# A hybrid transformer block: the second norm beside the attention, with its squares in two halves on ScalarE, its scaling on GpSimd and its transposes in groups of four

## The chip, the cores and the metric

The kernel runs on one core of one Trainium2 chip. The metric is the device time of one launch in microseconds (us). Every time below comes from the runs of the kernel before or from one profiled execution of it.

## The reference

One encoder block over 2048 tokens of width 1024, all in float32. What the change touches is the second norm, `h2`, and the attention that runs at the same time:

```python
h = rmsnorm(x, norm1_g) * (1.0 + sc1) + sh1
proj = h @ w_in                                  # 8 query heads, 2 key/value heads of 64, 512 pool channels
att = blocked_gqa(q, k, v)                       # softmax over all 2048 keys
pool = pool_mixer(u_pool, w_pool, pool_scale)
x = x + g1 * (jnp.concatenate([att, pool], -1) @ w_out)
h2 = rmsnorm(x, norm2_g) * (1.0 + sc2) + sh2     # y = x * rsqrt(mean(x*x) + 1e-6), per token
x = x + g2 * conv_gated_ffn(h2, w_up, conv_w, conv_b, w_down)
```

## The kernel before

The kernel has three stages: the first norm and the input projections (to about 380 us), the attention (380 to 1240 us), and the gated MLP (to the end). Matrices are split into a high and a low float32r part, so that most products take two or three matmuls.

**The attention** works through 32 *units*, numbered 0 to 31: a unit is one head for one chunk of 512 queries, chunk by chunk, 8 heads each. `gen_unit` goes over 16 key tiles. For each, TensorE makes a 128x512 tile of scores in PSUM with two matmuls (L731, and L732 which adds the row of maxima through `qb`), ScalarE takes the exponential twice (L735 into `ph`, L736 in place in PSUM), VectorE subtracts the two (L737, `pl`), and two tiles later TensorE multiplies by the values (L723 into bank `A`, L724 into bank `B`). GpSimd adds the `ph` of the first 13 tiles into `acc` (L739, then L741 eleven times). At the end of the unit ScalarE copies `acc` to `ah` (L751), VectorE makes its low part `al` (L752), and TensorE adds both into `B` (L757, L758); ScalarE and VectorE empty `A` and `B` (L765 to L768). For the next unit `gen_max` runs alongside: 16 matmuls (L692), each reduced by VectorE (L694), then the maxima as a row (L701), which ScalarE copies into `qb` (L702). The first L732 of a unit cannot start before that copy.

**Fillers.** Beside each unit a generator of other work is stepped at a fixed rate, which `count` (L913) sets: in units 8 to 15 the output projection (`gen_out`: matmuls L824, additions L846, loads L843, stores L847), in units 16 to 31 the second norm of token tiles 0 to 11 between further output projections. A scheduler then orders each engine's instructions by readiness, so a filler's instructions can stand some units before the place where they were written; the norm of tiles 0 and 1 starts in units 13 and 14.

**The second norm of a tile** (`ln2_early`, then `gen_ln2`, with 128 tokens): a load of x1 from DRAM into the buffer `l` (L879); ScalarE squares all 1024 columns and sums them (L853, an ACTIVATE and a short read of the accumulator); GpSimd makes the reciprocal root (L120, L121); VectorE scales the row in place (L857); a DMA copies it into a second buffer (L859); 8 transposes on TensorE into one PSUM bank, four at a time (L867), each four emptied by a ScalarE copy (L870) and stored (L871). Each buffer exists once, so the load of tile t+1 waits for the copy L859 of tile t, and that copy waits for the transposes of tile t-1. After `gen_ln2`'s first and second step come 4 and 8 empty steps (`LW`). Tiles 12 to 15 take the same function with `xr` None, in the turn from attention to MLP.

Every engine takes its own instructions strictly in order, and SyncE's queue (SP) issues all DMAs named here in order.

Of the kernel before, what the change touches and what calls it, by code (L numbers as in the profile page):

```python
# [10 lines left out]
F32 = mybir.dt.float32  # L11
F32R = mybir.dt.float32r
BF16 = mybir.dt.bfloat16
AF = mybir.ActivationFunctionType
ALU = mybir.AluOpType
# [3 lines left out]
P = 128  # L19
# [45 lines left out]
def hybrid_block(ctx: ExitStack, tc: tile.TileContext, x, c, w_ada, b_ada, norm1_g, w_in,  # L65
# [3 lines left out]
    V, S, G, PE, SP = nc.vector, nc.scalar, nc.gpsimd, nc.tensor, nc.sync  # L69

    x = x.rearrange("b t d -> (b t) d")
    out = out.rearrange("b t d -> (b t) d")
# [45 lines left out]
    def rstd_of(pool, ss, n, inv):  # L118
        r = pool.tile([P, n], F32, tag=f"rstd{n}", name="rstd", bufs=2)
        G.tensor_scalar(out=r, in0=ss, scalar1=inv, scalar2=EPS, op0=ALU.mult, op1=ALU.add)  # L120
        G.tensor_tensor(out=r, in0=r, in1=mhalf[:, 0:n], op=ALU.pow)  # L121
        return r
# [508 lines left out]
    with tc.tile_pool(name="po", bufs=1, side="right", reuse_waits="tile") as po, \  # L631
# [217 lines left out]
        def gen_ln2(t, x1, junk, hts, bank, stat, wait, xr=None):  # L849

            tok = t * P
            ss = stat.tile([P, 1], F32, tag="ss2", name=f"ss2{tok}", bufs=2)
            S.activation(out=junk(), in_=x1, func=AF.Square, accum_out=ss)  # L853
            r = rstd_of(stat, ss, 1, 1.0 / D)
            for _ in range(wait[0]):
                yield
            V.tensor_scalar(out=x1, in0=x1, scalar1=r, scalar2=None, op0=ALU.mult)  # L857
            if xr is not None:
                SP.dma_start(out=xr.bitcast(F32), in_=x1)  # L859
            for _ in range(wait[1]):  # L860
                yield
            src, eye = (x1, ident) if xr is None else (xr, identr)
            for q in range(2):
                tp = bank(f"tp2{tok}_{q}")
                for i in range(4):
                    k = q * 4 + i
                    PE.transpose(out=tp[:, i * P:(i + 1) * P], in_=src[:, k * P:(k + 1) * P], identity=eye)  # L867
                    yield
                hv = hts(q)
                S.copy(out=hv, in_=tp if xr is None else tp.bitcast(F32))  # L870
                SP.dma_start(out=h2_scr[4 * q:4 * q + 4, :, tok:tok + P].rearrange("k p t -> p k t"),  # L871
                             in_=hv.rearrange("p (k t) -> p k t", t=P))
                yield

        def ln2_early(t):
            xt, junk, xr, ht = (pw.tile([P, 2, QC], F32R, tag=f"mix{i}", name=f"l{i}_{t}", bufs=1)
                                .rearrange("p g t -> p (g t)") for i in ("00", "01", "10", "11"))
            xt, junk, ht = xt.bitcast(F32), junk.bitcast(F32), ht.bitcast(F32)
            SP.dma_start(out=xt, in_=x1_scr[t * P:(t + 1) * P])  # L879
            yield from gen_ln2(t, xt, lambda: junk, lambda q: ht[:, q * 512:(q + 1) * 512],  # L880
                               lambda nm: ps2.tile([P, 512], F32R, tag="misc", name=nm, bufs=1), p2, LW, xr)

        LW = (4, 8)
# [12 lines left out]
        def gen_first():  # L896
            mix3.extend(load_mix(NC - 1))
            for _ in range(12):
                yield
            yield from gen_tail_pool((("misc", 1), ("mx", 2), ("mx", 2)), mix3)  # L900
# [9 lines left out]
                2: lambda: chain(*(ln2_early(t) for t in range(4)), gen_out(1, 0), ln2_early(4), ln2_early(5)),  # L910
                3: lambda: chain(ln2_early(6), ln2_early(7), gen_out(2, 0), *(ln2_early(t) for t in range(8, 12)),
                                 gen_first())}
        count = {0: 2 * 96 + 12, 1: 192, 2: 96 + 6 * (10 + sum(LW)), 3: 96 + 6 * (10 + sum(LW)) + 48}  # L913
        filler = iter(())
        frac = 0.0
        FU, PT = 1, 1
# [151 lines left out]
        def gen_tail_att():  # L1068
            src = by_k(att.pop(NC - 1))
            for t in range(4):  # L1070
                tok = (NC - 1) * QC + t * P
                x1 = pv.tile([P, D], F32, tag=f"y{t}", name=f"x1{tok}", bufs=1)
                SP.dma_start(out=x1, in_=x[tok:tok + P])
                for n in range(2):
                    ns = slice(n * 512, (n + 1) * 512)
                    ps = tails[2 * t + n]
                    yield from gen_half(ps, src, 0, t, n, False, True)
                    V.tensor_tensor(out=x1[:, ns], in0=ps, in1=x1[:, ns], op=ALU.add)
                SP.dma_start(out=x1_scr[tok:tok + P], in_=x1)
                aux.append(gen_ln2(tok // P, x1, lambda: raw2("junk").bitcast(BF16),  # L1080
                                   lambda q: raw2("ht"), lambda nm: bank(nm), pa, TW[t]))
                step(aux[-1])

        def bank(nm):
            if ps3:
                return ps3[0].tile([P, 512], F32, tag="py", name=nm, bufs=3)
            return ps2.tile([P, 512], F32, tag="S", name=nm, bufs=3)
# [353 lines left out]
```

## Time and profile before

| | |
|---|---|
| median of 3 runs | 2693.97 us (2693.17 to 2694.17) |
| the profiled execution's own time | 2694.36 us |
| its span, first to last instruction | 2692.6 us |
| TensorE matmul busy | 2582.2 us, 96% of the span |
| VectorE busy | 1924.9 us, 71% |
| ScalarE busy | 1545.3 us, 57% |
| GpSimd busy | 1619.3 us, 60% |

The profiled execution is 0.39 us above the median, and 1.76 us of it lie outside the span. Matmul records overlap in time (each is shown from its start to its modelled end), so a busy share of 99% means that matmuls follow each other without a pause. In the records PE is TensorE, PEld its weight loads, DVE is VectorE, ACT is ScalarE, POOL is GpSimd, SPq SyncE's queue.

### The profile page before, as it was taken

What the parts mean: (1) busy time and instruction counts of PE and PEld (TensorE: products, weight loads), DVE (VectorE), ACT (ScalarE), POOL (GpSimd) and SP (SyncE); (2) the same over time, 40 slices, a digit from 0 to 9 for tenths busy, and PEclk for the clock granted to TensorE, in tenths of its full rate; (3) what the DMA queues carried; (4) which work ended last, traced back from release to release, by engine and by line L of the source; (5) the groups of instructions that cost most, each with busy time, mean ns of one, the idle gap of its engine ahead of it and who ended that gap; (6) DMA issues with size and microseconds to landing.
All of it is one profiled execution on the core that took longest, in us unless ns stands there. A gap on an engine that the chain in (4) does not pass through costs nothing.

```text
span 2692.6 us, 39012 instructions
## 1 busy us (share of the span) xinstructions
PE 2582.2 (96%) x13439; PEld 2238.4 (83%) x13439; DVE 1924.9 (71%) x3014; ACT 1545.3 (57%) x2848; POOL 1619.3 (60%) x1397
## 2 busy tenths in 40 slices
PE   5899989999999999999899999899999999999999
PEld 5788877777776777767898999799999997999998
DVE  7877678889988999897577776745555556455554
ACT  5565447767777778786654555554343445544442
POOL 1222135656566657574887887586565676777773
PEclk9899989999999999999999999999999999999999
DMA  9785373431223232333544444633333325333332
GB/s 293 237 265 180 97 240 101 153 100 58 69 73 98 64 100 62 97 110 120 172 149 134 149 130 140 197 106 102 106 105 95 94 78 189 114 122 118 107 112 87
DMA packets 320016, 344.90 MB, mean 128 GB/s; under 512 B 24975, under 2 KB 226649, under 8 KB 319817
## 3 DMA queue, kind: packets, MB, share of 16 engines
q1 hardware_dynamic: 318809, 338.60, 39.7%
q0 software_dynamic: 1008, 3.81, 0.5%
q8 instruction: 105, 1.72, 0.3%
q14 instruction: 94, 0.77, 0.1%
HBM read 249.42 MB, written 86.63 MB: 125 GB/s over the span
## 4 chain that ended last, share of the span: by engine, by line
PE 47%; DVE 2%; POOL 1%; ACT 1%; issue 1%; DMA 0%; DVEq 0%; SPq 0%; POOLq 0%; ACTq 0%
PE py L1254 16%; PE px L1165 13%; PE pw L1165 9%; PE pz L1165 8%; PE pl L1383 1%; DVE b L999 0%; POOL wl_s L1041 0%; ACT hb L983 0%; DVE y L1259 0%; DMA h_scr<-ht 0%; POOL wl_a L1041 0%; POOL t L1006 0%; POOL t L1013 0%; DMA hb<-h_scr 0%; DVE ac L1227 0%
## 5 line engine op out<-in xcount | busy, mean ns | idle before, releaser
L741 POOL TENSOR_TENSOR acc<-acc,ph 128x512 f32<-128x512 f32 x352 | 463.3, 1316 | 44.5 <-ACT ph L735 20.1
L1041 POOL TENSOR_TENSOR wl_s<-s,wh_s 128x512 fp32r<-128x512 f32 x260 | 349.4, 1345 | 204.7 <-ACT wh_s L1039 202.1
L735 ACT ACTIVATE ph<-S 128x512 fp32r<-128x512 f32 x512 | 306.8, 599 | 135.3 <-PE S L732 123.5
L737 DVE TENSOR_TENSOR pl<-S,ph 128x512 fp32r<-128x512 f32 x512 | 348.5, 684 | 40.5 <-ACT S L736 34.7
L1259 DVE TENSOR_TENSOR y<-py,y 128x512 f32<-128x512 f32 x300 | 205.9, 688 | 222.2 <-PE py L1254 220.6
L694 DVE TENSOR_REDUCE mx<-pmx 128x1 f32<-128x512 f32 x500 | 338.4, 681 | 21.1 <-PE pmx L692 19.5
L1039 ACT CAST wh_s<-s 128x512 fp32r<-128x512 f32 x264 | 163.5, 621 | 312.5 <-PE pw L1165 147.8
L1041 POOL TENSOR_TENSOR wl_a<-wr,wh_a 128x512 fp32r<-128x512 f32 x195 | 266.9, 1375 | 104.4 <-ACT wh_a L1039 104.0
L736 ACT ACTIVATE S<-S 128x512 f32<-128x512 f32 x512 | 306.0, 598 | 0.0
L1254 PE MATMUL py<-wdh,gh 128*128 128x512 f32 x664 | 261.7, 395 | 1.9 <-DVE y L1259 1.7
L1254 PE MATMUL py<-wdh,gl 128*128 128x512 f32 x664 | 262.0, 395 | 0.0
L1254 PE MATMUL py<-wdl,gh 128*128 128x512 f32 x664 | 261.8, 394 | 0.0
L1039 ACT CAST wh_a<-wr 128x512 fp32r<-128x512 f32 x198 | 122.3, 618 | 240.9 <-PE pz L1165 196.8
L1165 PE MATMUL px<-t,wh_s 128*128 128x322 f32 (+1 forms) x1024 | 248.0, 322 | 5.4 <-ACT p1s L1198 3.7
L724 PE MATMUL B<-pl,vt 128*128 128x512 f32 x512 | 209.9, 410 | 5.3 <-DVE pl L737 5.1
L732 PE MATMUL S<-qb,kB 65*128 65x512 f32 x512 | 203.3, 404 | 7.9 <-ACT qb L702 7.7
L692 PE MATMUL pmx<-kA,qa 128*128 128x512 f32 x500 | 204.9, 411 | 5.5 <-DMA kA<-k_scr 2.7
L723 PE MATMUL A<-ph,vt 128*128 128x512 f32 x512 | 204.4, 408 | 2.4 <-ACT ph L735 2.2
L731 PE MATMUL S<-qa,kA 128*128 128x512 f32 x512 | 202.7, 398 | 0.0
L1165 PEld LDWEIGHTS px<-t,wh_s 128*128 128x128 f32 x1024 | 178.3, 189 | 12.4 <-ACT p1s L1198 4.5
L739 POOL TENSOR_TENSOR acc<-ph,ph 128x512 f32<-128x512 f32 x32 | 41.2, 1288 | 239.2 <-ACT ph L735 209.2
L120 POOL TENSOR_SCALAR rstd<-ss 128x1 f32<-128x1 f32 (+1 forms) x48 | 20.5, 427 | 240.8 <-ACT junk L276 99.0
(297 smaller groups left out, 7034.4 us busy)
## 6 DMA issues: line engine op xcount, KB each, us to landing
wr<-in_w_up_dram SPq DMA_DIRECT2D x132, 512.0 KB
wdh<-wd_scr SPq DMA_DIRECT2D x88, 256.0 KB
wdl<-wd_scr SPq DMA_DIRECT2D x88, 256.0 KB
stage<-in_w_ada_dram SPq DMA_DIRECT2D x36, 512.0 KB
x_scr<-x SPq DMA_DIRECT2D x48, 256.0 KB
wds<-in_w_down_dram SPq DMA_DIRECT2D x44, 256.0 KB
wd_scr<-wdh SPq DMA_DIRECT2D x44, 256.0 KB
wd_scr<-wdl SPq DMA_DIRECT2D x44, 256.0 KB
```

Source lines behind the costliest of these rows:

```text
L692: PE.matmul(ps, qa[:, qt * P:(qt + 1) * P], kA[:, a, j * 512:(j + 1) * 512], start=True, stop=True)
L694: V.tensor_reduce(out=mx[:, qt, j:j + 1], in_=ps, axis=AX.X, op=ALU.max)
L724: PE.matmul(B, vt[:, kt, 64 + 64 * a:192 + 64 * a], pl, start=kt == 0, stop=False)
L735: S.activation(out=ph, in_=s, func=AF.Exp, scale=0.125)
L736: S.activation(out=s, in_=s, func=AF.Exp, scale=0.125)
L737: V.tensor_tensor(out=pl, in0=s, in1=ph.bitcast(F32), op=ALU.subtract)
L741: G.tensor_tensor(out=acc, in0=acc, in1=ph.bitcast(F32), op=ALU.add)
L1039: S.copy(out=hf, in_=src)
L1041: eng.tensor_tensor(out=lf, in0=src, in1=hf.bitcast(F32), op=ALU.subtract)
L1165: mm = PE.matmul(ps, l_[:, k], r_[:, k, 0:N], start=first and k == 0 and m == 0, stop=k == 3 and m == 2, skip_group_check=not first)
L1254: PE.matmul(ps, l_[:, ts_], r_, start=i == 0, stop=i == 3 * len(js) - 1)
L1259: V.tensor_tensor(out=ys[t][:, ns], in0=ps, in1=ys[t][:, ns], op=ALU.add)
```

## The change

For the twelve tiles beside the attention (`xr` not None) the squares are taken in two halves of 512 columns with two steps behind the first and one behind the second, and a GpSimd addition joins the two sums; the scaling moves from VectorE to GpSimd. For all 16 tiles the four transposes of a bank are issued in one step where each had a step of its own. A tile so takes 19 steps where it took 22, and `count`, from which the rate of the steps comes, follows. Lines from here on move by 10 in the changed kernel (L857 becomes L867, L879 becomes L889).

```diff
         def gen_ln2(t, x1, junk, hts, bank, stat, wait, xr=None):
 
             tok = t * P
-            ss = stat.tile([P, 1], F32, tag="ss2", name=f"ss2{tok}", bufs=2)
-            S.activation(out=junk(), in_=x1, func=AF.Square, accum_out=ss)
+            if xr is None:
+                ss = stat.tile([P, 1], F32, tag="ss2", name=f"ss2{tok}", bufs=2)
+                S.activation(out=junk(), in_=x1, func=AF.Square, accum_out=ss)
+            else:
+                s2, j2 = stat.tile([P, 2], F32, tag="ss2h", name=f"ss2h{tok}", bufs=2), junk()
+                for i in range(2):
+                    hs = slice(512 * i, 512 * (i + 1))
+                    S.activation(out=j2[:, hs], in_=x1[:, hs], func=AF.Square, accum_out=s2[:, i:i + 1])
+                    for _ in range(2 - i):
+                        yield
+                ss = s2[:, 0:1]
+                G.tensor_tensor(out=ss, in0=ss, in1=s2[:, 1:2], op=ALU.add)
             r = rstd_of(stat, ss, 1, 1.0 / D)
             for _ in range(wait[0]):
                 yield
-            V.tensor_scalar(out=x1, in0=x1, scalar1=r, scalar2=None, op0=ALU.mult)
+            (V if xr is None else G).tensor_scalar(out=x1, in0=x1, scalar1=r, scalar2=None, op0=ALU.mult)
...
                 for i in range(4):
                     k = q * 4 + i
                     PE.transpose(out=tp[:, i * P:(i + 1) * P], in_=src[:, k * P:(k + 1) * P], identity=eye)
-                    yield
+                yield
...
-        count = {0: 2 * 96 + 12, 1: 192, 2: 96 + 6 * (10 + sum(LW)), 3: 96 + 6 * (10 + sum(LW)) + 48}
+        count = {0: 2 * 96 + 12, 1: 192, 2: 96 + 6 * (7 + sum(LW)), 3: 96 + 6 * (7 + sum(LW)) + 48}
```

The order of the instructions is the same up to unit 12 and differs in small ways to the end of the turn into the MLP. Three places matter to the prediction.

*The end of unit 13.* First SyncE's queue, before and now (`l_1` with four digits is the x1 buffer of tile 1, `qa` and `qb` are query loads of unit 16, `o` and `rc` the row sums of unit 13):

```order
L847 DMA x_scr<-x_1_0_8178 128x512
L843 DMA x_1_0_8444<-x_scr 128x512
L680 DMA qa_8183<-q_scr 128x512
L681 DMA qb_8184<-q_scr 64x512
L879 DMA l_1_9241<-x_scr 128x1024
L774 DMA r_scr<-o_8429 1x512
```

```order
L847 DMA x_scr<-x_1_0_8178 128x512
L843 DMA x_1_0_8444<-x_scr 128x512
L889 DMA l_1_9230<-x_scr 128x1024
L680 DMA qa_8183<-q_scr 128x512
L681 DMA qb_8184<-q_scr 64x512
L847 DMA x_scr<-x_0_0_8327 128x512
```

Then ScalarE at the same place, before and now:

```order
L751 CAST ah_8407<-acc_8148 128x512
L765 COPY o_8429<-A_8149 64x512
L766 COPY o_8429<-B_8150 1x512
L853 ACTIVATE l_1_9242,ss_9246<-l_1_9241 128x1024
L702 CAST qb_7587<-row_8414 1x512
L735 ACTIVATE ph_0_8454<-S_0_8451 128x512
```

```order
L751 CAST ah_8407<-acc_8148 128x512
L765 COPY o_8429<-A_8149 64x512
L859 ACTIVATE l_1_9231,ss2h_9235<-l_1_9230 128x512 x2
L702 CAST qb_7587<-row_8414 1x512
L766 COPY o_8429<-B_8150 1x512
L735 ACTIVATE ph_0_8454<-S_0_8451 128x512
```

The load of tile 1 stands two DMAs earlier. Both halves of its squares stand one behind the other; before and now they are ahead of the copy into `qb`, and now they are also ahead of the copy of bank `B`.

*The end of unit 15*, ScalarE, before and now (tile 2):

```order
L765 COPY o_9002<-A_8745 64x512
L870 COPY l_1_9244<-tp_0_9357 128x512
L870 COPY l_1_9244<-tp_1_9406 128x512
L766 COPY o_9002<-B_8746 1x512
L853 ACTIVATE l_2_9456,ss_9460<-l_2_9455 128x1024
L702 CAST qb_8184<-row_8989 1x512
L735 ACTIVATE ph_0_9020<-S_0_9017 128x512
```

```order
L765 COPY o_9002<-A_8745 64x512
L880 COPY l_1_9233<-tp_0_9375 128x512
L880 COPY l_1_9233<-tp_1_9410 128x512
L859 ACTIVATE l_2_9432,ss2h_9436<-l_2_9431 128x512
L766 COPY o_9002<-B_8746 1x512
L702 CAST qb_8184<-row_8989 1x512
L859 ACTIVATE l_2_9432,ss2h_9436<-l_2_9431 128x512
L735 ACTIVATE ph_0_9020<-S_0_9017 128x512
```

One half now stands ahead of the copy of bank `B`, the other behind the copy into `qb`.

*The end of unit 16*, GpSimd, before and now (`acc_9014` is unit 16's):

```order
L120 TENSOR_SCALAR rstd<-ss_9663 128x1
L121 TENSOR_TENSOR rstd<-rstd,mhalf 128x1
L741 TENSOR_TENSOR acc_9014<-acc_9014,ph_8_9146 128x512
L741 TENSOR_TENSOR acc_9014<-acc_9014,ph_9_9162 128x512
L741 TENSOR_TENSOR acc_9014<-acc_9014,ph_10_9180 128x512
L741 TENSOR_TENSOR acc_9014<-acc_9014,ph_11_9198 128x512
L802 TENSOR_TENSOR attl_7126<-att_8898,atth_7125 128x512
L741 TENSOR_TENSOR acc_9014<-acc_9014,ph_12_9214 128x512
```

```order
L741 TENSOR_TENSOR acc_9014<-acc_9014,ph_11_9198 128x512
L863 TENSOR_TENSOR ss2h_9639<-ss2h_9639 128x1
L120 TENSOR_SCALAR rstd<-ss2h_9639 128x1
L121 TENSOR_TENSOR rstd<-rstd,mhalf 128x1
L867 TENSOR_SCALAR l_3_9634<-l_3_9634,rstd 128x1024
L802 TENSOR_TENSOR attl_7126<-att_8898,atth_7125 128x512
L741 TENSOR_TENSOR acc_9014<-acc_9014,ph_12_9217 128x512
```

The scaling of tile 3 stands ahead of unit 16's last addition. Of the twelve scalings seven stand in the gap behind a unit's last addition and five within a unit's additions: in units 16 (tile 3, before the last one), 19 (tile 4, after the ninth), 23 (tile 7, after the tenth), 26 (tile 8, after the fifth) and 29 (tile 11, after the seventh).

## Rows read from the trace of the kernel before

**Rows 1.** Windows: busy us (instructions) of PE, PEld, DVE, ACT, POOL; clock; DMA share, GB/s

```profile
440.00:735.00 295.00, 291.90 (x1258) 228.52 (x1258) 267.04 (x438) 215.75 (x401) 179.89 (x138) 1.00 0.32 100
735.00:970.00 235.00, 226.29 (x957) 169.62 (x956) 212.06 (x349) 179.10 (x337) 147.13 (x121) 0.98 0.28 82
970.00:1200.00 230.00, 221.81 (x958) 164.12 (x956) 209.15 (x348) 182.80 (x348) 145.31 (x120) 1.00 0.32 97
```

**Rows 2.** Timeline, unit 13 into 14: start, us, engine, line, operation [idle before <-releaser]

```profile
759.80 0.32 SPq L843 DMA_DIRECT2D x<-x_scr  x1
...
762.29 1.69 SPq L879 DMA_DIRECT2D l<-x_scr  x1
...
765.34 0.39 PE L758 MATMUL B<-al,onesr 128*128 128x512 f32 x1
...
767.84 1.06 ACT L853 ACTIVATE l<-l 128x1024 f32<-128x1024 f32 x1 [1.50 <-DMA l<-x_scr]
...
769.01 0.57 ACT L702 CAST qb<-row 1x512 fp32r<-1x512 f32 x1
...
769.64 0.73 PE L732 MATMUL S<-qb,kB 65*128 65x512 f32 x2 [1.93 <-ACT qb L702]
```

**Rows 3.** Windows, the stretches behind the two long stalls

```profile
769.70:773.40 3.70, 3.70 (x11) 2.90 (x12) 3.42 (x7) 3.09 (x6) 1.69 (x3) 0.61 0.20 68
826.00:831.00 5.00, 5.00 (x12) 3.45 (x12) 4.52 (x8) 3.09 (x6) 2.55 (x2) 0.50 0.30 109
```

**Rows 4.** Timeline, unit 15 into unit 16

```profile
818.07 0.50 SPq L879 DMA_DIRECT2D l<-x_scr  x1
...
822.17 0.69 DVE L768 TENSOR_TENSOR o<-B,o 64x512 f32<-64x512 f32 x1 [1.04 <-ACT o L766]
...
823.64 0.50 PE L692 MATMUL pmx<-kA,qa 128*128 128x512 f32 x1 [1.77 <-DVE mx L694]
823.91 1.06 ACT L853 ACTIVATE l<-l 128x1024 f32<-128x1024 f32 x1 [1.77 <-DMA l<-x_scr]
...
825.09 0.57 ACT L702 CAST qb<-row 1x512 fp32r<-1x512 f32 x1
...
825.71 1.65 PE L732 MATMUL S<-qb,kB 65*128 65x512 f32 x3 [1.56 <-ACT qb L702]
...
828.22 1.27 POOL L739 TENSOR_TENSOR acc<-ph,ph 128x512 f32<-128x512 f32 x1 [2.25 <-ACT ph L735]
```

**Rows 5.** Waits, 735 to 1200 us: us in total, times, longest

```profile
PE S L732 <- ACT qb L702: 7.1, 7, 1.9
```

**Rows 6.** Groups by line: busy us, mean ns | idle before

```profile
L741 POOL TENSOR_TENSOR acc<-acc,ph 128x512 f32<-128x512 f32 x352 | 463.3, 1316 | 44.5 <-ACT ph L735 20.1
L857 DVE TENSOR_SCALAR l<-l,rstd 128x1024 f32<-128x1024 f32 x12 | 9.2, 767 | 6.7 <-POOL rstd L121 6.5
L736 ACT ACTIVATE S<-S 128x512 f32<-128x512 f32 x512 | 306.0, 598 | 0.0
L102 POOL MEMSET onesz<- 128x192 f32 x1 | 0.3, 253 | 0.0
```

**Rows 7.** Timeline, the last addition and the copy `ah`: units 16, 19 and 23

```profile
846.84 1.29 POOL L741 TENSOR_TENSOR acc<-acc,ph 128x512 f32<-128x512 f32 x1
848.46 0.64 ACT L751 CAST ah<-acc 128x512 fp32r<-128x512 f32 x1
...
921.99 1.29 POOL L741 TENSOR_TENSOR acc<-acc,ph 128x512 f32<-128x512 f32 x1
923.83 0.61 ACT L751 CAST ah<-acc 128x512 fp32r<-128x512 f32 x1
...
1025.28 2.66 POOL L741 TENSOR_TENSOR acc<-acc,ph 128x512 f32<-128x512 f32 x2
1028.23 0.60 ACT L751 CAST ah<-acc 128x512 fp32r<-128x512 f32 x1
```

**Rows 8.** Timeline, the turn into the MLP: the first transpose of tile 12

```profile
1282.67 0.47 PE L867 MATMUL tp<-ident,x 128*128 128x128 f32 x1 [5.27 <-DVE x L857]
```

## The prediction

> **What bounds the kernel now.** I read the windows first, because the change lives between 735 and 1200 us. In the attention before it TensorE is busy for 291.90 of 295 us, with 1258 matmuls in that time, 0.232 us each [rows 1]: there it is the bound. In the two stretches with the second norm it is busy for 226.29 of 235 and 221.81 of 230 us: 8.7 and 8.2 us without a matmul, where the first stretch's rate would leave 2.5 each. Some 12 us of pauses, and a clock of 0.98 in the first stretch, are all that this part has to give. VectorE stands at 90% to 91% in all three, so it is close behind TensorE, and ScalarE and GpSimd are below 80%: what delays TensorE there is order and latency more than any engine's sum.
>
> Then the timeline, for where the pauses are. Two are long. **Unit 13 into 14** [rows 2]: the load of tile 1 is issued at 762.29; ScalarE, with the squares next in its queue, waits 1.50 us for it, squares from 767.84, and only at 769.01 copies the row into `qb`; TensorE stands 1.93 us until the first L732. The granted clock is 0.61 in the next 3.7 us [rows 3], so 0.39 x 3.7 = 1.4 us of TensorE's time go as well. **Unit 15 into 16** [rows 4]: the same with tile 2, where ScalarE waits 1.77 us, TensorE 1.77 and then 1.56 us, and the clock is 0.50 for 5 us [rows 3], the lower of TensorE's two levels (1.2 GHz of 2.4): another 2.5 us. The waits by group show that L732 waited for `qb` seven times, 7.1 us in all [rows 5]; without the two long ones (1.93 and 1.56) five remain, with 3.6 us together.
>
> Last, who is late at a unit's end. In unit 16 GpSimd's last addition ends at 846.84 + 1.29 = 848.13 and the copy `ah` starts at 848.46; the gaps are 0.33 us there, 0.55 in unit 19 and 0.29 in unit 23 [rows 7]. In these units GpSimd's chain of 12 additions already sets the end.
>
> **The change, part by part.** Durations are from the profiled execution, and the sum is made against its 2694.36 us, which is 0.39 above the median.
>
> *Squares at unit 14.* The load now follows L843, issued at 759.80 + 0.32, so some 2.1 us earlier than 762.29; with the same 5.55 us to the squares (762.29 to 767.84) the data are there at about 765.7. A half is priced by the 128x512 exponential, 0.60 us [rows 6], and 0.1 for the read of the sum (767.84 to 769.01 is 1.17 for a square of 1.06): 0.70, two of them 1.4. `qb` then starts at 767.1 and L732 at 767.7, 1.9 us earlier. But TensorE has four matmuls fewer ahead of that L732 than before (three where seven stood), 0.93 us that it must do later: the pause shrinks by 1.0, to about 0.95. Does the clock still fall? The five short waits, 0.7 us each, did not lower it (four of them lie in the second stretch of [rows 1], at 1.00), 1.93 us did; 0.95 is nearer to the short ones, so I take three quarters of the 1.4. Term: **-2.1 us**; ends: 0 (the load is no earlier) and -3.4 (pause and clock loss gone).
>
> *Squares at unit 16.* The load of tile 2 waits for the copy of tile 1, and that for tile 0's transposes, which now end about one key tile sooner (three units from 848.46 to 923.83 [rows 7], 18 steps each: 1.4 us): the data at 822.5 instead of 823.91. Then the first half (0.70), the copy of `B` (0.57, as the copy into `qb`), VectorE's L768 (0.69) and the reduction behind it (as long) stand in line before the L692 that TensorE must do ahead of L732. That L692 comes at about 825.1, where it came at 823.64, and L732 at 825.4 instead of 825.71: one wait takes the place of another. At the unit's end the scaling of tile 3 stands ahead of GpSimd's last addition. Term: **0**; ends: -5.8 (the pauses of 3.3 and the clock's 2.5 vanish) and +1.4 (the scaling's upper price below).
>
> *Fillers at the other starts of units.* In the order of the changed kernel three of the five short waits have two or three projection matmuls or four transposes ahead of L732: 3 x 0.7 = 2.2 us; as these units are not bound by TensorE throughout, two thirds: **-1.4** (ends 0 and -2.2).
>
> *Scaling off VectorE.* 12 x 0.767 = 9.2 us of VectorE's time go [rows 6]. In units full of projection matmuls TensorE hides them. Six tiles (2, 3, 6, 7, 10, 11) lie in units with few of them, 4.6 us; since a unit waits by turns for VectorE, ScalarE and GpSimd there, a third: **-1.5** (ends 0 and -4.6).
>
> *Scaling on GpSimd.* No row shows a GpSimd operation with one input of 1024 columns. Above, two inputs at 1.316 us for 512 columns make 2.63 [rows 6]; below, VectorE's own 0.767; GpSimd's fill of 192 columns in 0.253, in proportion, makes 1.35. A scaling streams one tensor, as the fill does, so I take 1.3. Seven scalings stand in the gap behind a unit's last addition, where GpSimd waits for the next unit's exponentials in any case (2.25 us at 828.22 [rows 4]); they cost nothing while they fit. Of the five within a unit's additions two have slack to spare, unit 16 is counted above, and in units 19 and 23 the addition of sums (0.2) and the scaling exceed the gaps: 0.2 + 1.3 - 0.55 = 1.0 and 0.2 + 1.3 - 0.29 = 1.2. In unit 28 the root moves behind the last addition, about -0.6. Term: **+1.6**; at 2.63 it is 1.3 more in each of the two and 1.0 in unit 29, +5.2.
> The Trainium skill (GPSIMD Engine Reference, section 4.1, Engine selection) speaks against the move: elementwise work on a tile belongs on VectorE, GpSimd being about twice as slow with two inputs and roughly at line rate with one. Twice VectorE's duration, an estimate by that page, is 1.53 us and would add 0.5 us to the sum; line rate would take 1.1 us off. No run here shows which holds.
>
> *Squares in two pieces.* 12 x (1.4 - 1.17) = 2.8 us more for ScalarE; it is last in perhaps a third of these units: **+0.9** (ends 0 and 2.8).
>
> *Grouped transposes.* In the order before, most transposes of a bank already stood by threes and fours, so nothing is counted (ends 0 and -1). In the turn into the MLP the first transpose of tile 12 waits 5.27 us for VectorE's L857 [rows 8], which is not changed, and the groups only come nearer to it: 0 (ends -2 and +2). What must also stay hidden: the copy L869 now waits in SyncE's queue for GpSimd instead of VectorE, with the row sums' DMAs behind it; late row sums would stop VectorE at L798.
>
> Sum: -2.1 + 0 - 1.4 - 1.5 + 1.6 + 0.9 = -2.5. 2694.36 - 2.5 = 2691.9, as a median **2691.5 us**: no change that a measurement could tell, as that takes about 0.2%, 5.4 us.
>
> **The rivals.** *Both long pauses go.* If the loads land before ScalarE comes to the squares, unit 14 gives 3.4, the short waits 2.2, VectorE 2.5; unit 16 gives 3.5 of its 5.8 before GpSimd's chain holds it: -11.6 + 1.6 + 0.9 = -9.1, a median of 2684.9. For it: both pauses begin with a wait for a load, and the order moves one load up. Against: tile 2's load stands at the same place in its queue, and the first half now delays the copy of `B`. Chance 0.36.
>
> *GpSimd's chain becomes the end of the units.* With the scaling near 2.63 us the terms are +1.4 (unit 16), +5.2 and, as ScalarE's copy `ah` then waits with the halves ahead of it, the full +2.8; the gains shrink to 1.0, 1.0 and 0.5: +6.9, a median of 2700.9. Three units follow the scaling's price one for one, so the sum is zero from about 2.1 us on. For it: gaps of 0.3 us, and the price of all two-input rows. Against: one input. Chance 0.22.
>
> *The halves do not interleave.* For tiles 0, 1 and 9 the scheduler put both in one place, so that they stop ScalarE for 1.4 us where one square took 1.17. That lies in the forecast's terms; if it were so everywhere, the first term falls away: 2693.6, still no change.
>
> **How the numbers follow.** No change has 0.42 (the forecast with the last case), faster 0.36, slower 0.22. The range 2682 to 2700 takes in the first rival with some room for the unit-16 term, and stops just short of the second's middle; the forecast's own is 2688 to 2697.
>
> **What would show it.** In the changed profile: the wait of L732 at the start of unit 14 near 1 us and full clock behind it; at the start of unit 16 L692 waiting for a reduction until after the copy of `B`, and a low clock still; the GpSimd TENSOR_SCALAR at 1.0 to 1.6 us; `ah` close behind the last addition in units 16, 19 and 23; TensorE's busy share in 735 to 1200 us at 97%. A scaling over 2 us, or a unit 16 under 27 us, would make the forecast wrong, to either side.

## The result, and the profile after

The changed kernel takes 2718.68 us as the median of four runs (2717.22 to 2720.07), against 2693.57 us for the kernel before on the same chip: a ratio of 1.0096, 95% interval 1.0084 to 1.0109. It is slower by some 25 us, outside the range of the forecast.

Four views of the changed kernel show where. First the windows, the stretches of [rows 1] and [rows 3] and two new ones (busy us (instructions) of PE, PEld, DVE, ACT, POOL; clock; DMA share, GB/s):

```profile
440.00:735.00 295.00, 292.65 (x1268) 229.49 (x1267) 267.17 (x441) 215.31 (x400) 179.65 (x138) 1.00 0.33 101
735.00:970.00 235.00, 221.49 (x938) 163.69 (x937) 206.76 (x339) 178.07 (x345) 161.26 (x130) 0.99 0.27 81
970.00:1200.00 230.00, 212.53 (x908) 160.80 (x908) 196.82 (x322) 174.03 (x340) 153.97 (x127) 0.96 0.29 86
...
1014.80:1021.60 6.80, 4.41 (x13) 3.36 (x14) 2.27 (x5) 2.02 (x5) 2.44 (x3) 0.50 0.43 157
1038.70:1045.50 6.80, 3.86 (x11) 3.06 (x12) 1.62 (x4) 1.19 (x2) 0.80 (x1) 0.50 0.40 135
...
769.70:773.40 3.70, 3.66 (x17) 2.70 (x16) 3.50 (x6) 3.50 (x8) 3.60 (x3) 1.00 0.38 132
826.00:831.00 5.00, 4.91 (x19) 3.18 (x19) 3.97 (x7) 3.62 (x8) 4.92 (x3) 1.00 0.22 88
```

The attention before the second norm is as it was. In the two stretches with the norm TensorE now stands for 13.5 and 17.5 us instead of 8.7 and 8.2. The two places with a low clock of [rows 3] are at full clock; in their stead the clock is 0.50, the lower of TensorE's two levels, in places such as 1014.8 and 1038.7 us. Next the groups by line between 735 and 1230 us (busy us, mean ns | idle before, and what ended it):

```profile
L867 POOL TENSOR_SCALAR l<-l,rstd 128x1024 f32<-128x1024 f32 x12 | 34.6, 2887 | 1.2
L877 PE MATMUL tp<-identr,l 128*128 128x128 f32 x96 | 16.0, 257 | 20.9 <-DMA l<-l 20.5 <-ACT l L880 0.3
L859 ACT ACTIVATE l<-l 128x512 f32<-128x512 f32 x24 | 15.1, 630 | 2.4 <-DMA l<-x_scr 2.4
```

The scaling takes 2.89 us on GpSimd, 3.8 times VectorE's 0.767 [rows 6] and above the forecast's upper bound of 2.63. And TensorE stands 20.9 us at the transposes L877, nearly all of it for the copy `l<-l` (L869) that brings the scaled row into the transposes' buffer. The second longest of these stops (4.89 us in unit 23; the longest is 4.99 in unit 16), in the timeline:

```profile
1031.72 0.63 ACT L859 ACTIVATE l<-l 128x512 f32<-128x512 f32 x1
1032.23 0.21 ACT L859 ACTIVATION_READ_ACCUMULATOR l<-l 128x1 f32 x1
1034.19 0.19 POOL L863 TENSOR_TENSOR ss2h<-ss2h 128x1 f32<-128x1 f32 x1
...
1035.41 2.86 POOL L867 TENSOR_SCALAR l<-l,rstd 128x1024 f32<-128x1024 f32 x1
1038.23 1.26 POOL L741 TENSOR_TENSOR acc<-acc,ph 128x512 f32<-128x512 f32 x1
1038.30 0.49 SPq L869 DMA_DIRECT2D l<-l  x1
1039.53 0.62 ACT L751 CAST ah<-acc 128x512 fp32r<-128x512 f32 x1 [2.07 <-POOL acc L741]
...
1041.64 0.34 PE L877 MATMUL tp<-identr,l 128*128 128x128 f32 x1 [4.89 <-DMA l<-l]
```

The squares of tile 7 are summed at 1032.44. GpSimd adds the halves only at 1034.19, as additions of `acc` stand ahead in its queue; root and scaling end at 1038.27; the copy, issued at once, is there 3.3 us later. TensorE, whose next instruction is the transpose, stands all the while, with the unit's last matmuls behind it, and its clock is 0.50 from 1038.7 on.

In unit 19 there are no transposes, and GpSimd's chain alone can be read (where [rows 7] had `ah` 1.84 us behind the start of the last addition, 0.55 of it slack):

```profile
922.42 2.86 POOL L867 TENSOR_SCALAR l<-l,rstd 128x1024 f32<-128x1024 f32 x1
925.24 3.96 POOL L741 TENSOR_TENSOR acc<-acc,ph 128x512 f32<-128x512 f32 x3
926.54 0.60 ACT L735 ACTIVATE ph<-S 128x512 fp32r<-128x512 f32 x1 [2.19 <-POOL acc L741]
...
929.24 0.62 ACT L751 CAST ah<-acc 128x512 fp32r<-128x512 f32 x1 [0.27 <-POOL acc L741]
```

The slack is used up: `ah` starts 0.04 us behind the last addition's end (925.24 + 3.96 = 929.20). An exponential waits 2.19 us for a `ph` buffer that an addition behind the scaling must free. Last, the place that the change was to mend, unit 13 into 14, to be set beside [rows 2]:

```profile
762.52 0.38 SPq L889 DMA_DIRECT2D l<-x_scr  x1
...
767.26 0.63 ACT L859 ACTIVATE l<-l 128x512 f32<-128x512 f32 x1
...
767.89 0.61 ACT L859 ACTIVATE l<-l 128x512 f32<-128x512 f32 x1
...
768.09 0.45 PE L758 MATMUL B<-al,onesr 128*128 128x512 f32 x1
...
768.63 0.57 ACT L702 CAST qb<-row 1x512 fp32r<-1x512 f32 x1
...
769.36 0.40 PE L732 MATMUL S<-qb,kB 65*128 65x512 f32 x1
```

L732 now starts 1.27 us behind L758 (769.36 - 768.09), where it was 4.30 (769.64 - 765.34 in [rows 2]): the pause is gone. By units (from one L758 to the next) unit 14 went from 30.20 to 27.47 us. Against that, unit 13 grew by 1.85 us, unit 16 from 30.19 to 33.82, unit 19 from 24.12 to 26.41, unit 23 from 24.29 to 36.82 and unit 29 from 26.54 to 35.20; the others together gave 3.7 us back.

### The profile page after: what moved, and what is told of

It reads as the page before. It is cut to its first block, busy times and chain, and to the rows that moved or that the text cites. A ratio compares the mean times of both kernels' runs of the same rounds, so it can differ in the third digit from the quotient of the medians.

```text
span 2718.3 us, 39068 instructions
## 1 busy us (share of the span) xinstructions
PE 2587.3 (95%) x13439; PEld 2241.6 (82%) x13439; DVE 1921.9 (71%) x3002; ACT 1548.0 (57%) x2872; POOL 1653.0 (61%) x1421
## 4 chain that ended last, share of the span: by engine, by line
PE 47%; DVE 2%; ACT 1%; POOL 1%; issue 1%; DMA 0%; DVEq 0%; ACTq 0%; POOLq 0%
PE py L1264 15%; PE px L1175 13%; PE pw L1175 9%; PE pz L1175 8%; PE pl L1393 1%; DVE b L1009 0%; ACT hb L993 0%; POOL wl_s L1051 0%; POOL t L1016 0%; DVE y L1269 0%; DMA h_scr<-ht 0%; POOL t L1023 0%; DVE t L1009 0%; DVE ac L1237 0%; DVE wds L56 0%
## 5 line engine op out<-in xcount | busy, mean ns | idle before, releaser
L732 PE MATMUL S<-qb,kB 65*128 65x512 f32 x512 | 203.5, 403 | 3.7 <-ACT qb L702 3.4
L1175 PE MATMUL px<-t,wl_s 128*128 128x322 f32 (+1 forms) x512 | 163.9, 320 | 0.0
```

Of the source, the lines that this page charges most:

```text
L1175: mm = PE.matmul(ps, l_[:, k], r_[:, k, 0:N], start=first and k == 0 and m == 0, stop=k == 3 and m == 2, skip_group_check=not first)
```

## The experiments

Each kernel was timed against the kernel before on its own chip (medians of before there: 2687.64 to 2689.12 us for the experiments, 2693.57 for the change); ratios are given with their 95% intervals, and kernels of different chips are compared by them. The part ahead of unit 12, which hardly any edit touches, ended between 698.8 and 711.8 us in the profiles, so single profiles are compared from there: "attention" is from unit 11's last L758 to unit 31's, "turn" from there to the first down projection of the MLP. What follows, to the end of the span, takes 1360.4 to 1361.2 us in every kernel. A stop is time in which TensorE stands before a transpose of the second norm.

```
kernel                    ratio to before           attention   turn   stops at transposes (us)
before                    1                           528.4     92.2     0.4
the change                1.0096 [1.0084, 1.0109]     551.0     94.3    20.9
scale_on_vector       e1  1.0014 [1.0004, 1.0025]     533.1     92.9     3.1
only_gpsimd_scale     e2  1.0103 [1.0087, 1.0118]     552.1     92.3     3.4
only_halves           e3  1.0006 [0.9995, 1.0017]     528.6     92.6     0.5
only_groups           e4  1.0020 [1.0010, 1.0029]     528.0     93.9     0.6
extra_op              e5  1.0050 [1.0037, 1.0063]     538.0     92.4     0.3
half_each             e6  1.0022 [1.0012, 1.0032]     533.0     93.8     3.0
later_transposes      e7  1.0117 [1.0102, 1.0132]     553.6     96.2    17.6
scale_on_scalar       e8  1.0031 [1.0020, 1.0042]     534.1     92.8     0.9
held_transposes       e9  1.0041 [1.0029, 1.0054]     538.7     94.0     0.2
held_on_vector       e10  1.0026 [1.0017, 1.0036]     532.1     93.4     0.4
two_scalings         e11  1.0130 [1.0114, 1.0146]     561.1     94.6    24.6
alone_held           e13  1.0030 [1.0020, 1.0041]     534.8     92.2     0.1
alone_low_part       e14  1.0068 [1.0054, 1.0082]     542.0     92.4     2.5
low_part_control     e15  1.0041 [1.0027, 1.0054]     533.0     92.3     0.2
groups_in_turn       e16  1.0002 [0.9992, 1.0011]     526.8     93.0     0.3
```

The attention as one window of the trace, in the order before, the change, e2, e9, e10 (columns as in the windows above):

```profile
710.90:1239.30 528.40, 510.75 (x2179) 381.99 (x2177) 473.71 (x779) 412.39 (x778) 337.54 (x278) 0.99 0.28 84
711.80:1262.80 551.00, 514.28 (x2183) 384.87 (x2180) 472.01 (x767) 415.24 (x802) 373.06 (x302) 0.98 0.27 81
709.20:1261.30 552.10, 520.23 (x2185) 391.03 (x2183) 468.95 (x767) 414.75 (x778) 370.53 (x290) 0.97 0.26 81
707.40:1246.10 538.70, 512.47 (x2177) 384.87 (x2175) 469.17 (x767) 417.67 (x802) 373.57 (x302) 0.98 0.27 83
698.80:1230.90 532.10, 507.96 (x2178) 381.57 (x2176) 476.06 (x779) 416.99 (x802) 340.42 (x290) 0.99 0.27 84
```

TensorE has nearly as many matmuls in each (2177 to 2185), and stands for 17.7, 36.7, 31.9, 26.2 and 24.1 us. So of the 22.6 us that the change loses in the attention 19.1 are standing, and 3.5 are matmuls that take longer, at a mean clock of 0.98 instead of 0.99. Of e2's 23.7 us 14.2 are standing and 9.5 are matmuls that take longer, at 0.97: a stop also costs by the clock behind it.

### Which part of the change: e1 to e4

e1, the change with its scaling back on VectorE:

```diff
-            (V if xr is None else G).tensor_scalar(out=x1, in0=x1, scalar1=r, scalar2=None, op0=ALU.mult)
+            V.tensor_scalar(out=x1, in0=x1, scalar1=r, scalar2=None, op0=ALU.mult)
```

> The whole change, but the scaling of the twelve tiles stays on VectorE (halves and groups kept). Theory A (the scaling takes 2.89 us on GpSimd, stands in its queue among the additions, so the copy into the transposes' buffer is late and TensorE stops at the transposes): the stops at L877 of 5.4, 10.0 and 8.1 us in units 16, 23 and 29 go to under 2 us each, and the time falls from 2718.7 to 2690 us, between 2684 and 2698. Theory B (the group of four transposes stops TensorE in one piece): the stops stay, 2710 to 2720 us. Theory C (the second half of the squares comes two steps later and the root with it): half of the stops stay, about 2705 us.

e2, the kernel before with that line alone changed the other way:

```diff
-            V.tensor_scalar(out=x1, in0=x1, scalar1=r, scalar2=None, op0=ALU.mult)
+            (V if xr is None else G).tensor_scalar(out=x1, in0=x1, scalar1=r, scalar2=None, op0=ALU.mult)
```

> The kernel before, with nothing but the scaling of the twelve tiles moved from VectorE to GpSimd. Theory A: 12 scalings of 2.86 us on GpSimd, TensorE stops at the transposes again or the copy `ah` is late in units 16, 19 and 23, and the time is 2705 to 2720 us. Theories B and C: nearly the time before, 2690 to 2699 us, since squares and transposes are as they were.

e3 and e4 are the kernel before with the diff's halves alone (and 13 for 10 in `count`) and its groups alone (4 for 10).

> The kernel before, with nothing but the squares of the twelve tiles in two halves with their three steps (the steps counted in the rate), scaling on VectorE, transposes one to a step. Theory A: 2688 to 2697 us, the long pauses before L732 at units 14 and 16 shorter. Theory B: the same. Theory C: 2700 to 2712 us.

> The kernel before, with nothing but the four transposes of a bank in one step (the steps counted in the rate). Theory A: 2690 to 2698 us, with at most the 2.6 us by which the turn into the MLP became longer. Theory B: 2705 to 2720 us, with stops at L867 in units 16, 23 and 29. Theory C: as A.

Medians: 2692.45, 2714.73, 2689.35 and 2693.87 us, with 2689.12 for the kernel before. The move of the scaling is nearly the whole loss: alone it costs 25.6 us, and without it the change is 3.3 us over the kernel before (with one new stop of 2.65 us at the transposes, in unit 22). B and C fall. (By the trace the change's stops in units 16, 23 and 29 are 5.1, 8.5 and 7.0 us, not the 5.4, 10.0 and 8.1 of the expectations, and e2's 3.4, not the 2.6 of later ones.) A has a crack, though: in e2 TensorE stands only 3.4 us at the transposes, and loses as much. It stands elsewhere, as in unit 24 of e2, in the timeline:

```profile
1043.79 12.69 POOL L741 TENSOR_TENSOR acc<-acc,ph 128x512 f32<-128x512 f32 x9
...
1053.62 0.39 PE L824 MATMUL po<-wo,atth 128*128 128x512 f32 x1
...
1056.44 1.26 POOL L802 TENSOR_TENSOR attl<-att,atth 128x512 fp32r<-128x512 f32 x1
1057.75 0.80 PE L824 MATMUL po<-wo,attl 128*128 128x512 f32 x1 [3.75 <-POOL attl L802]
```

Here TensorE waits 3.75 us for `attl`, the low part that GpSimd makes behind its additions. GpSimd is no later with it than in the kernel before: in both traces L802 starts 20.6 us behind the start of the L758 that opens the unit, and no scaling stands in this unit. It is the matmul L824 that stands earlier: its first use of `attl` behind this L802 comes 24.4 us into the unit in the kernel before, and TensorE stands ready for it at 18.2 us here.

### What the scaling costs by its size: e5, e6, e8, e11, e12

e5 leaves the scaling on VectorE and puts as long an operation into GpSimd's queue; e6 halves it; e8 gives it to ScalarE; e11 cuts it in two (with 8 for 7 in `count`). The lines shown are those for the twelve tiles; tiles 12 to 15 keep VectorE.

```diff
 e5, on the kernel before, behind VectorE's scaling
+                jk = junk()
+                G.tensor_scalar(out=jk, in0=jk, scalar1=r, scalar2=None, op0=ALU.mult)
 e6, on the change
+                V.tensor_scalar(out=x1[:, 0:512], in0=x1[:, 0:512], scalar1=r, scalar2=None, op0=ALU.mult)
+                G.tensor_scalar(out=x1[:, 512:1024], in0=x1[:, 512:1024], scalar1=r, scalar2=None, op0=ALU.mult)
 e8, on the change
+                S.activation(out=x1, in_=x1, func=AF.Identity, scale=r)
 e11, on the change, for i = 0 and 1, with a yield behind the first
+                    G.tensor_scalar(out=x1[:, hs], in0=x1[:, hs], scalar1=r, scalar2=None, op0=ALU.mult)
```

> The kernel before, unchanged in its scaling on VectorE, with one more GpSimd operation behind each root: the same TENSOR_SCALAR of 128x1024 by the root, on the dead buffer of the squares, so that nobody waits for its result but the next tile's squares. It keeps GpSimd's queue for 2.86 us at the place where the moved scaling stood. Theory A1 (the copy into the transposes' buffer is late, because the scaling itself is late): the time before, 2688 to 2694 us. Theory A2 (the 2.86 us in GpSimd's queue hold up what stands behind them, the additions and the low part `attl`): most of the loss of the scaling moved alone (25.6 us), 2705 to 2716 us.

> The whole change, but GpSimd scales only 512 of the 1024 columns (1.45 us by the row of 2.86) and VectorE the other 512. If the loss goes in proportion to GpSimd's time: half of the way from 2692.5 (scaling on VectorE) to 2718.7, about 2705 us. If GpSimd's chain has slack that the whole scaling exceeds and the half does not (my price of 1.3 us, of which the forecast made +1.6 us): 2692 to 2697 us.

> The whole change, but the scaling is done by ScalarE (1.06 us by the row of the whole square, 12 times). Neither VectorE nor GpSimd has it then. If VectorE's 9.2 us were worth 1.5 us, as the forecast said, and ScalarE hides its own: about 2691 us, against 2692.5 with the scaling on VectorE. If ScalarE, which has the exponentials, is as little free as GpSimd: 2698 to 2706 us.

> The whole change, with the scaling on GpSimd in two operations of 512 columns, one step apart (1.43 to 1.67 us each), so that additions can stand between them. If the length of one blocking operation is what costs: near the run with half of the columns, 2695 to 2702 us. If GpSimd's added time as a whole costs, as both theories A say: 2712 to 2722 us.

Medians: 2701.08, 2694.35 and 2696.55 us for e5, e6 and e8, with 2687.64 for the kernel before, and 2724.02 for e11, with 2688.47. An operation that nobody waits for costs 13.4 us (9.6 in the attention): units 19, 23, 28 and 29, in which it stands among the additions, are 1.8 to 2.2 us longer each. So A2 is real, yet gives only half. Half a scaling, 1.67 us on average, costs 0.08% over e1, 2.2 us, which the intervals don't tell from nothing (in the attention 533.0 us against 533.1), where the whole one costs 0.82%: the loss isn't in proportion. But that is not the size alone. With half a scaling the transposes stand at the places of e1 (the table below), with e1's stops; so whether GpSimd's chain has a threshold isn't shown. Cut in two, with the transposes at the places of the change, it is worse than whole, so the length of a single operation is not the cause; GpSimd's time rose to 37.5 us and the stops at the transposes to 24.6. ScalarE instead of VectorE gains nothing.

e12 prices GpSimd's operations on the dead buffer of the squares, two tiles for each form (one execution, read for its durations alone):

```diff
 on the kernel before, behind VectorE's scaling; f = t % 6, a_ and b_ the halves of jk
+                if f == 0:
+                    G.tensor_scalar(out=jk, in0=jk, scalar1=0.5, scalar2=None, op0=ALU.mult)
...
+                elif f == 3:
+                    G.tensor_copy(out=b_, in_=a_)
```

> The kernel before with one more GpSimd operation per tile on the dead buffer of the squares, of six forms, two of each: the scaling of 1024 columns by a constant; 512 columns by the root in place; 512 by the root into the other half; a copy of 512; a product of two operands of 512; a fill of 1024. The forecast's price (one input streams at the fill's rate, 1.3 ns a column) says: 1.35, 0.68, 0.68, 0.68, 1.31, 1.35 us. If a one-input operation costs per column what the two-input addition costs (2.56 ns): 2.6 to 2.9, 1.3 to 1.45, the same, the same, 1.3, and the fill 1.35.

By tile and form (duration in ns, shortest/median/longest, first and last start):

```profile
L863 POOL TENSOR_SCALAR l<-l x2: 2781/2786/2792, 737.5 to 1001.6; 128x1024 f32<-128x1024 f32 x2
L865 POOL TENSOR_SCALAR l<-l,rstd x2: 1572/1847/2122, 771.9 to 1018.7; 128x512 f32<-128x512 f32 x2
L867 POOL TENSOR_SCALAR l<-l,rstd x2: 1574/1845/2116, 825.8 to 1090.7; 128x512 f32<-128x512 f32 x2
L869 POOL COPY l<-l x2: 607/608/609, 838.3 to 1113.2; 128x512 f32<-128x512 f32 x2
L871 POOL TENSOR_TENSOR l<-l x2: 1296/1296/1296, 913.8 to 1151.3; 128x512 f32<-128x512 f32 x2
L873 POOL MEMSET l<- x2: 952/952/952, 947.9 to 1177.5; 128x1024 f32 x2
```

Per column: fill 0.93 ns (952/1024), copy 1.19 (608/512), product of two operands 2.53 (1296/512), scaling 2.72 (2786/1024) by a constant, 3.07 (1572/512) by the root. The second sample of each scaling of 512 columns took 2.12 us; what lengthened it isn't known. Not the number of inputs sets the price here but arithmetic against moving: a scaling with one input is as dear as a product with two, in place or not.

### TensorE's order: e7, e9, e10

The place of each tile's first transpose in TensorE's order, as unit.key tile (for tiles 2, 3, 6, 7, 10 and 11; the others hardly differ, but for e9, where they too stand 5 to 19 key tiles later than with the change):

```
                   tile 2   tile 3   tile 6   tile 7   tile 10  tile 11
before              16.4     17.4     23.4     24.4     29.4     29.16
the change          16.10    16.16    23.3     23.16    29.0     29.14
e1 scale_on_vector  17.4     18.4     23.4     24.4     29.4     29.16
e2 only scaling     16.8     16.16    22.16    23.11    28.16    29.8
e6 half each        17.4     18.4     23.4     24.4     29.4     29.16
e7 later            16.10    16.16    23.3     23.16    28.16    29.10
e9 held             17.16    18.12    24.10    25.0     29.7     29.16
```

With the slower scaling the scheduler puts tile 7's transposes four key tiles earlier than with the quick one, and tile 3's four (before) or twenty (e1): it orders by its own reckoning of when things are ready. More empty steps (e7) don't bind it; an edge to the instruction written before (e9, and e10 with the scaling on VectorE) does.

```diff
 e7
-        LW = (4, 8)
+        LW = (4, 14)
 e9 on the change, e10 on e1
-                    PE.transpose(out=tp[:, i * P:(i + 1) * P], in_=src[:, k * P:(k + 1) * P], identity=eye)
+                    tr = PE.transpose(out=tp[:, i * P:(i + 1) * P], in_=src[:, k * P:(k + 1) * P], identity=eye)
+                    if xr is not None and i == 0:
+                        tc.keep_in_program_order(tr)
```

> The whole change, with 14 empty steps instead of 8 between the scaling and the transposes (the rate follows). Theory A1: the stops of 5.4, 10.0 and 8.1 us at the transposes shrink to under 2 us each, and the time is 2692 to 2700 us. Theory A2: the stops at the transposes shrink, but TensorE stops at other lines instead, and the time stays at 2708 to 2718 us.

> The whole change, but the first transpose of each bank is held behind everything written before it on TensorE, which more empty steps alone did not do: the transposes now stand 4 to 18 key tiles later in TensorE's order (tile 3 after the third key tile of unit 17 instead of the end of unit 16, tile 7 at the start of unit 25 instead of the end of unit 23). Theory A1 (what costs is that TensorE stops at transposes whose copy is late): the stops go and with them nearly all of the 25 us, 2692 to 2697 us. Theory A2 (what costs is GpSimd's queue itself): the stops go and the time stays at 2703 to 2716 us, as the scaling alone in the kernel before cost 25.6 us with 2.6 us of stops at the transposes, and the extra operation that nobody waits for cost 13.4.

> The same held transposes, with the scaling on VectorE: the control for the run before. If the holding itself costs nothing, 2690 to 2694 us, as without it (2692.5); if the later stores and loads of a tile delay the next tiles, up to 2700 us. The difference to the run before is then what GpSimd's queue costs by itself.

e7, at 2719.35 us, tells nothing on A1: in units 16 and 23 the transposes stayed where they were, and so did the stops (5.0 and 8.5 us). e9 does what e7 was meant to do. Its groups by line in 735 to 1250 us:

```profile
L867 POOL TENSOR_SCALAR l<-l,rstd 128x1024 f32<-128x1024 f32 x12 | 34.3, 2859 | 1.2
L877 PE MATMUL tp<-identr,l 128*128 128x128 f32 x96 | 12.5, 246 | 0.2 <-ACT l L882 0.2
```

The scaling is as long as in the change, the stops are gone, and the median is 2701.07 us, 12.6 over the kernel before. With the scaling on VectorE under the same holding it is 2694.65. So the scaling on GpSimd costs 6.4 us with the transposes held (6.6 in the attention; by the ratios 4.0), and 22 us where the scheduler places them (the change's 25.1 us over the kernel before less e1's 3.3; by the ratios 0.82%, the same). Some 15 of the 22 us go when the transposes stand later, with the scaling as long as it was; by the ratios it is 18 of 22, in the attention 11.3 of 17.9. So e9 lies between its two expectations: most of the price is A1's.

What is left isn't GpSimd's chain alone. Of the 6.6 us between e9 and e10 in the attention unit 26 has 5.1; units 19, 23 and 29 have 1.1 together. Unit 26 in e9:

```profile
1094.05 2.86 POOL L867 TENSOR_SCALAR l<-l,rstd 128x1024 f32<-128x1024 f32 x1
...
1096.93 0.49 SPq L869 DMA_DIRECT2D l<-l  x1
1097.48 0.59 SPq L778 DMA_DIRECT2D rb<-r_scr  x1
...
1100.76 0.69 DVE L798 TENSOR_TENSOR att<-o,rb 64x512 f32<-64x512 f32 x1 [3.17 <-DMA rb<-r_scr]
...
1102.82 0.50 PE L724 MATMUL B<-pl,vt 128*128 128x512 f32 x1 [2.83 <-DVE pl L737]
```

The copy L869 is issued when the scaling ends (1094.05 + 2.86 = 1096.91), and the load of the row sums `rb` right behind it. VectorE waits 3.17 us for them at L798, with the subtraction that TensorE needs behind that, and TensorE stands 2.83 us. With 125 matmuls in unit 26 of both kernels, that stop and 1.9 us of longer matmuls (clock 0.95 in e9, 1.00 in e10) are most of the 5.1. In e2, e13 and e14 VectorE waits at L798 for `rb` too, 2.8, 4.2 and 2.8 us in all; in the kernel before, the change and e10 it doesn't.

### The scaling alone once more: e13 to e16

e13 is e2 with e9's holding; e14 is e2, and e15 the kernel before, with `attl` on VectorE; e16 groups only the transposes of tiles 12 to 15.

```diff
 e14, e15
-        E1, E2 = V, G
+        E1, E2 = V, V
 e16, on the kernel before
-                    yield
+                    if xr is not None:
+                        yield
+                if xr is None:
+                    yield
```

> The kernel before with only the scaling on GpSimd (which alone cost 25.6 us, with only 2.6 us of stops at the transposes), and the first transpose of each bank held behind everything written before it on TensorE. If the loss comes from the places that TensorE's order gives to the norm's work and to what shares its PSUM bank (the output projection), too early for so long a scaling: 5 to 14 us over the kernel before. If it comes from GpSimd's queue whatever the order on TensorE: 20 to 27 us over.

> The kernel before with only the scaling on GpSimd, and with the low part `attl` (L802, 16 operations of 1.26 us on GpSimd behind a unit's additions) moved from GpSimd to VectorE. If TensorE's stops before the output projection of 3.9 and 3.8 us in units 24 and 30, which waited for `attl`, are a cause of their own: 7 to 10 us less than with the scaling alone, so 2703 to 2708 us by its 2714.7. If they only stand where another wait would: under 4 us less.

> The control for the run before: the kernel before, scaling on VectorE, with `attl` on VectorE. VectorE has 16 operations of about 0.7 us more, GpSimd 16 of 1.26 less. Either way 0 to 5 us over the kernel before; a gain would say that GpSimd's queue is the bound in the kernel before already.

> The kernel before with the transposes in groups of four only for the tiles 12 to 15, in the turn from the attention into the MLP. In the profiles the turn took 92.2 to 92.6 us without groups and 92.8 to 94.3 with them (one with groups: 96.2). If the loss of the grouping alone (ratio 1.0020) lies in the turn: 1.0010 to 1.0020. If it lies in the attention: within 0.0007 of 1.

Medians: 2698.42, 2708.52, 2700.60 and 2690.29 us, with 2688.41 for the kernel before. Holding the transposes takes the price of the scaling alone from 25.6 to 10.0 us (from 23.7 to 6.4 in the attention, as in e9 against e10). With `attl` off GpSimd the scaling costs 7.9 us over its control instead of 25.6 (9.0 in the attention instead of 23.7). But the control e15 is itself 12.2 us over the kernel before, where 0 to 5 were expected (4.6 of them are in the attention; where the others lie isn't shown), and e14 is 20.1 over it. So moving `attl` saves 5.5 us of e2's 25.6 by the medians and 9.4 by the ratios. In e2 TensorE waits 6.5 us for `attl` (3.75 in unit 24, 2.76 in unit 30), and behind the first of these the clock is 0.55 for 6.8 us. So the places in TensorE's order are the larger part of e2's loss as well, by e13; that `attl` is most of it isn't shown. The two remedies overlap, and how much of e2 belongs to which of them stays open. The groups cost nothing in the turn alone (e16); why e4 is 0.2% slower isn't settled, since its single profile is 0.4 us shorter in the attention and 1.7 longer in the turn.

No kernel was faster than the kernel before; the halves alone (e3) and the groups in the turn (e16) can't be told from it.

## Why the prediction was wrong

**The step that failed** is the scaling on GpSimd, twice. "A scaling streams one tensor, as the fill does, so I take 1.3": it takes 2.89 us. The bound above, two inputs at the addition's rate, was not an upper end either; e12 shows that one input is no argument, as a scaling costs 2.7 to 3.1 ns a column and a fill 0.93. The Trainium skill (GPSIMD Engine Reference, section 4.1, Engine selection) has one-input work on GpSimd roughly at line rate: this case's trace says otherwise for the scaling, 3.8 times VectorE's duration; only the copy comes nearer (1.19 ns a column, 1.6 times VectorE's 0.75 in its scaling [rows 6]).

**The size of that step.** At the price that the forecast took nothing speaks against its +1.6: e6, at 1.67 us, costs 2.2 us over e1, but with intervals that reach from a gain to 6 us, and with nothing in the attention. At the full price the rival "GpSimd's chain becomes the end of the units" had 1.4 us in unit 16, 2.3 and 2.5 in units 19 and 23 and 1.0 in unit 29 (6.6 with a gain of 0.6 in unit 28). e5, which lengthens GpSimd's queue and nothing else, is 1.1, 2.2, 1.8 and 2.1 us longer there, and 2.2 in unit 28: so the rival's mechanism is shown, near its price. That the kernels with the transposes held give 6.4 us, nearly the same 6.6, is luck: the units that the rival named have little of it, and unit 26 alone 5.1 us, most of them from the wait for the row sums.

**What no step had.** The term "Grouped transposes" says that "in the order before, most transposes of a bank already stood by threes and fours, so nothing is counted". It looks at the transposes among themselves. Their places relative to the scaling were to be read from the order as well: with the change they stand at the end of unit 16 and of unit 23 instead of four key tiles into the next. TensorE waited there for the copy L869; holding them back takes the stops from 20.9 to 0.2 us and most of the 22 us with them. Under "what must also stay hidden" the forecast saw that this copy waits for GpSimd, with the row sums behind it in SyncE's queue, and priced it at nothing. In the change that held; in e9 it is most of the 5.1 us of unit 26.

**The other terms.** *Squares at unit 14*, -2.1: near; the pause went, where 0.95 us of it was to stay, the clock is 1.00 in 769.7 to 773.4 us, and unit 14 is 2.7 us shorter. But 1.85 came back in unit 13, where tile 0's scaling stands ahead of the unit's additions. *Unit 16*, 0: the low clock behind its start went, against the forecast, as the first rival said; TensorE then lost 5 us and more at the transposes of tile 3. *Other starts of units*, -1.4, and *scaling off VectorE*, -1.5: not found. e3 shows where such gains go (by units and their matmuls, [rows 4] being the start of the first): units 16 and 17 are 3.0 us shorter with 186 matmuls where 206 stood, and units 18 and 19 are 3.3 us longer with 222 where 202 stood: the work that filled a pause only moves. And e8, with neither VectorE nor GpSimd scaling, is no faster than e1. *Squares in two pieces*, +0.9: two halves take 1.37 us (767.26 to 768.63), as forecast, and e3 as a whole is 0.2 us over the kernel before. *Grouped transposes*, 0: within the forecast's bounds in the attention and in the turn by their profiles, though e4 as a whole is 0.2% slower, more than these say.

Of the two signs of a wrong forecast, a scaling over 2 us came and a unit 16 under 27 us did not: unit 16 took 33.8 us. TensorE's busy share in the two stretches is 93% (221.49 + 212.53 of 465 us), where 97% was to show it. The forecast's chance of slower, 0.22, was on the case that happened, but that rival's middle, 2700.9 us, already lay above the range, and the 17.8 us from there to 2718.68 are what neither had, in the main the order on TensorE.

## What to carry to other kernels

When an operation moves to a slower engine, look up who consumes its result and where that consumer stands in its own engine's order: an in-order engine that is given the consumer too early stands still with everything behind it, and here that cost about twice as much as all else that the slower scaling brought (15 against 6 us by the medians, 11 against 7 in the attention). Look also at what stands behind its copy in the DMA queue: a copy that waits for the slower engine holds up the transfers behind it. Price an operation by a row of the same operation on that engine, or run one; here rows of fills and copies said nothing of arithmetic. Where a scheduler orders by its own reckoning, empty steps in the program need not delay an instruction (e7); an explicit order edge did (e9).

## What the runs showed of the hardware

GpSimd takes 2.79 us for a float32 scaling of 128x1024 by a constant, 1.30 for a product of two 128x512 operands, 0.61 for a copy of 512 columns and 0.95 for a fill of 1024 (e12): by column multiplying costs more than twice what copying does, with one operand or two. TensorE's clock fell to 0.50 during its stops of 3.6 and 4.9 us in unit 23, and stayed at 1.00 behind the stop of 1.87 us at the start of unit 16, where the kernel before, with 1.77 and 1.56 us in close succession [rows 4], had fallen to 0.50.
